# One order of steps for a whole two-layer backbone: single PSUM banks in the first stage, and both plain output projections written as steps

## The chip, the cores and the metric

The kernel runs on one core of a Trainium2 chip. The core has a matrix engine (TensorE, "PE" in the profile, with "PEld" for its weight loads), VectorE ("DVE"), ScalarE ("ACT"), GpSimd ("POOL"), and queues that start transfers; most of them are issued by the core's sync engine ("SP"). The on-chip memory SBUF holds tiles of 128 partitions; the matrix engine writes to PSUM, which has eight banks of 128 x 512 float32 numbers. The metric is the device time of one execution in microseconds, and fewer is better.

## The reference: what is computed

512 latent tokens and 256 context tokens, 1024 wide, pass through two layers. Layer 0 mixes tokens by windowed attention (16 query heads and 4 key/value heads of width 64, a sink logit per head, a band of 384 keys and the 256 context keys). Layer 1 mixes them by a gated MLP over chunks of 128 tokens. Behind each mixer stands a SwiGLU feed-forward net (FFN) of hidden width 2816. Both halves of a layer stand between RMS norms and are modulated by six rows (shift, scale and gate for mixer and FFN), which come from SiLU of a conditioning vector times a 1024 x 6144 matrix. Shortened:

```python
mod_l = silu_c @ ada_w[i] + ada_b[i]           # six rows of 1024
h_l = modulate(rmsnorm(x, norm_g[i, 0]), sh_ml, sc_ml)
y_l = mixer(h_l, h_c)                          # layer 0: attention @ a_w_o, layer 1: (u * mixed) @ b_w_o
x = x + g_ml * rmsnorm(y_l, norm_g[i, 1])
f_l = swiglu(modulate(rmsnorm(x, norm_g[i, 2]), sh_fl, sc_fl), ffn_w_in[i], ffn_w_out[i])
x = x + g_fl * rmsnorm(f_l, norm_g[i, 3])
```

The context tokens feed only the keys and values of layer 0, since layer 1 does not read them.

## The kernel before

**Arithmetic.** Nearly every product is taken from halves: an operand is cast to a reduced format on ScalarE (`high`, line 403: "hi"), the rest is formed by a subtraction on VectorE or GpSimd (`low`, line 410: "lo"), and three matmuls hi x hi, hi x lo, lo x hi are added in PSUM. Weights come in 88 units of 1 MB (`Stream`, `ws`): `ws.fetch` brings a unit into one of two raw buffers, `ws.high` and `ws.low` form its halves in four pairs of tiles `w_hi`, `w_lo`.

**Stages.** First stage: the six token tiles (tiles 0 to 3 latent, 4 and 5 context) are loaded, normed and transposed (`turn_in`, line 683), shift and scale of the mixer are worked out per block of 128 channels (`ada0_rows`, `ada0_cols`), and keys and values are summed over eight such blocks (`kv`, line 763). Tables for the rotary embedding are loaded (`rope_in`) and transposed (`rope_turn`, line 904). Then the keys are copied out, rotated, transposed and split into halves (`k_copy`, `k_rope`, `k_add`, `k_turn`, `k_split`, lines 977 to 1018), the values are copied out (`v_copy`), and two of the eight query projections are made (`q_first`). Attention runs in 16 blocks of 128 queries and one key/value head; the other query projections, and the first half (four blocks of channels) of the output projection for token tiles 2 and 3 (`wo_high`, `wo_low`, `wo_part`), stand among them.

Then the output projection (`down`, line 1363): weight units 6 to 9, four token tiles, each with a chain behind it (`Chain`: square, rstd, gain, add to x, norm, shift, transpose) that leads to the hidden state H of the FFN. The FFN (`FFN`) makes its first two units plainly (`head`) and the other 20 as seven products of quarters in place of eight (`product`, line 1609; sums and differences of quarters by `diff` and `sum_a`). Its output matrix is done likewise (`seven`, line 1836: `product7`, `add7`, and `plain7` for what is left over). Layer 1 follows with the gated MLP (`v_part`, `u_part`, `mixed`), a second call of `down`, and the second FFN, whose end stores the result. Beside all this the modulation rows are summed on VectorE from chunks of the 1024 x 6144 matrices (`Ada`; in the names of the steps `m` and the row's number, 0 to 5, with `#2` where a name comes a second time, for layer 1).

**What sets the order of work.** Every engine takes its instructions in the order in which the program issues them. Most of the program is given as named steps, `at(time, step, ...)` (line 780); `run_plan` (line 790) sorts the steps planned so far and issues them. A step whose name stands in the long list `ORDER` is issued at its place there; any other falls behind, by its time. Inside `tc.manual_schedule()` that order is kept; outside of it the framework's own planner sorts instructions by a simulated timeline. Before, two stretches lay outside: the loads of x for layer 0's residual, and in both calls of `down` the first two weight units (the halves of their weights, `staged` halves of their inputs, their matmuls and a generator `bg` that adds up one modulation row). A tile that is released and taken anew makes the new writer wait for the last reader.

**PSUM in the first stage.** Three slots of two banks (`slotA`) and two single banks (`bankA`) share the eight banks. A pair of token tiles has its keys and values in one slot, and the four heads' transposed keys of a pair take one slot.

## Time and profile before

| What | us |
|---|---|
| median of three runs | 1098.92 (1098.61 to 1098.96) |
| the profiled execution's own time | 1098.0 |
| its span | 1096.2 |
| TensorE busy | 1078.7 |
| VectorE busy | 943.3 |
| ScalarE busy | 607.7 |
| GpSimd busy | 260.6 |

The span runs from the first to the last instruction of the profiled execution; its own time lies 1.8 us above the span. Matmuls overlap, and the profile models their ends, so a gap between two of them shows only where it is longer than the overlap. In a row of a group stand the line, the engine, the operation, output <- inputs, shapes and count, then the busy time and the mean of one in ns, then the idle time before it and what ended it. In a row of a timeline stand the start, the time taken and the instruction, and in brackets the idle time before it.

### The profile page before, as it was taken

Reading aid. Unit: us, or ns where it says so; the run is one execution under the profiler, and the core shown is the slowest. Engines: PE = TensorE matmul, PEld = TensorE weight load, DVE = VectorE, ACT = ScalarE, POOL = GpSimd, SP = SyncE. Lnnn points to the kernel's source line nnn. Section 1 sums busy time; section 2 is a strip of 40 time slices with the busy share of each in tenths; the row PEclk is TensorE's granted clock in tenths of the full one; section 3 lists DMA queues with packets and bytes.
Section 4 is the critical chain, followed back from the end, with each engine's and each line's share of the span. In section 5 each row is a group of like instructions: output and inputs, shape, how many; then the busy total and the mean of one; then the engine's idle time right before and its main releaser. Section 6 shows DMA issues by size and latency. Waiting matters only on the chain.

```text
span 1096.2 us, 17751 instructions
## 1 busy us (share of the span) xinstructions
PE 1078.7 (98%) x6894; PEld 948.6 (87%) x6894; DVE 943.3 (86%) x1386; ACT 607.7 (55%) x1054; POOL 260.6 (24%) x268
## 2 busy tenths in 40 slices
PE   8999999999999999999999999999999999999997
PEld 5778777878899999998888888888999999998885
DVE  6798999859999999978988778878988888979975
ACT  6447778656645555555665434356555554555662
POOL 2417767525500000001322311007300000003400
PEclk9999999999999999999999999999999999999999
DMA  9746342433255655459953387651243344369811
GB/s 367 278 164 182 114 146 75 136 127 111 82 174 191 193 176 183 162 174 312 227 95 116 111 303 277 204 191 48 77 154 135 103 149 154 123 229 307 166 22 77
DMA packets 50393, 181.25 MB, mean 165 GB/s; under 512 B 5371, under 2 KB 9723, under 8 KB 39173
## 3 DMA queue, kind: packets, MB, share of 16 engines
q1 hardware_dynamic: 42756, 165.44, 43.5%
q0 software_dynamic: 7552, 14.68, 7.8%
q8 instruction: 54, 0.88, 0.3%
q14 instruction: 31, 0.25, 0.1%
HBM read 171.71 MB, written 2.10 MB: 159 GB/s over the span
## 4 chain that ended last, share of the span: by engine, by line
PE 86%; DVE 7%; DMA 2%; issue 2%; ACT 1%; POOL 1%; SPq 1%; DVEq 0%; POOLq 0%; ACTq 0%
PE f L1618 35%; PE y L1802 14%; PE y L1829 5%; PE y L467 4%; PE v L467 4%; PE s_ps L1095 3%; PE pT_ps L1128 3%; PE o_ps L1144 2%; PE q_ps L856 2%; PE u L2038 1%; PE u L2036 1%; PE u L2037 1%; PE kv L459 1%; PE q L856 1%; PE kv L461 1%
## 5 line engine op out<-in xcount | busy, mean ns | idle before, releaser
L1618 PE MATMUL f<-H,w_hi 128*128 128x256 f32 x960 | 178.4, 284 | 1.1 <-DVE fc L1629 0.5
L1618 PEld LDWEIGHTS f<-H,w_hi 128*128 128x128 f32 x960 | 149.8, 192 | 2.2 <-DVE fc L1629 1.4
L1618 PE MATMUL f<-H,w_lo 128*128 128x256 f32 x480 | 135.8, 283 | 0.0
L1802 PE MATMUL y<-w_hi,s 128*128 128x512 f32 x448 | 120.1, 389 | 0.0
L1618 PE MATMUL f<-S,w_hi 128*128 128x256 f32 x640 | 118.7, 283 | 0.0
L403 ACT CAST w_hi<-w_raw 128x1024 fp32r<-128x1024 f32 x90 | 94.5, 1052 | 33.6 <-PE y L1802 7.8
L403 ACT CAST w_hi<-T 128x1024 fp32r<-128x1024 f32 x80 | 83.7, 1047 | 50.8 <-PE f L1618 33.2
L410 DVE TENSOR_TENSOR w_lo<-w_raw,w_hi 128x1024 fp32r<-128x1024 f32 (+1 forms) x81 | 96.3, 1198 | 7.8 <-ACT w_hi L403 5.8
L1625 ACT COPY fc<-f 128x256 f32<-128x256 f32 x120 | 44.8, 373 | 103.7 <-PE f L1618 101.2
L1618 PEld LDWEIGHTS f<-S,w_hi 128*128 128x128 f32 x640 | 99.9, 192 | 0.0
L1802 PEld LDWEIGHTS y<-w_hi,s 128*128 128x128 f32 x448 | 84.1, 188 | 17.4
L410 DVE TENSOR_TENSOR w_lo<-T,w_hi 128x1024 fp32r<-128x1024 f32 x80 | 97.4, 1217 | 0.0
L1618 PEld LDWEIGHTS f<-H,w_lo 128*128 128x128 f32 x480 | 92.1, 192 | 0.0
L1618 PE MATMUL f<-S,w_lo 128*128 128x256 f32 x320 | 90.7, 283 | 0.0
L1790 POOL DMA_DIRECT2D t<-in_w x48 | 42.3, 939 | 182.9 <-DMA t<-in_w 116.7
L583 POOL DMA_DIRECT2D acc<-acc x8 | 6.9, 866 | 313.0 <-DVE acc L569 307.2
L569 DVE SCALAR_TENSOR_TENSOR acc<-ada_k,sc,acc 128x1024 f32<-128x1024 f32 x56 | 71.6, 1279 | 7.5 <-DMA ada_k<-in_ada 5.3
L1802 PE MATMUL y<-w_lo,s 128*128 128x512 f32 x224 | 69.0, 389 | 0.0
L1618 PE MATMUL f<-H,x 128*128 128x256 f32 x480 | 64.2, 283 | 0.0
L467 PE MATMUL y<-w_hi,st 128*128 128x512 f32 x224 | 62.4, 391 | 0.0
L1618 PEld LDWEIGHTS f<-S,w_lo 128*128 128x128 f32 x320 | 61.4, 192 | 0.3 <-DVE w_lo L410 0.3
L1618 PEld LDWEIGHTS f<-H,x 128*128 128x128 f32 x480 | 60.5, 192 | 0.1
(257 smaller groups left out, 2750.0 us busy)
## 6 DMA issues: line engine op xcount, KB each, us to landing
w_raw<-in_w SPq DMA_DIRECT2D x67, 1024.0 KB, 5.9
ada_k<-in_ada SPq DMA_DIRECT2D x56, 512.0 KB, 4.6
ada_raw<-in_ada SPq DMA_DIRECT2D x12, 1024.0 KB, 4.9
w<-in_w SPq DMA_DIRECT2D x12, 1024.0 KB, 9.3
t<-in_w POOLq DMA_DIRECT2D x48, 256.0 KB, 5.9
ada<-in_ada SPq DMA_DIRECT2D x8, 1024.0 KB, 8.4
t<-in_w SPq DMA_DIRECT2D x8, 1024.0 KB, 13.6
w_raw<-in_w SPq DMA_DIRECT2D x10, 512.0 KB, 4.1
```

The costliest lines, as they stand in the source:

```text
L403: nc.scalar.copy(out=hi, in_=src)
L410: (eng or nc.vector).tensor_tensor(out=v(lo), in0=v(src), in1=v(hi).bitcast(F32), op=ALU.subtract)
L467: nc.tensor.matmul(dst, l, w[:, n * 512:(n + 1) * 512], start=first and i == 0, stop=last and i == 2)
L569: nc.vector.scalar_tensor_tensor(out=self.acc, in0=self.raws.pop(k), scalar=sc[:, k:k + 1], in1=self.acc, op0=ALU.mult, op1=ALU.add)
L856: nc.tensor.matmul(q_ps[p], w, HA[:, x, :], start=k == 0 and i == 0, stop=k == KC - 1 and i == 2)
L1095: nc.tensor.matmul(dst, q, keys, start=i == 0, stop=i == 1)
L1128: nc.tensor.transpose(ps[:, j * P:(j + 1) * P], self.probs[j][:, i * P:(i + 1) * P], ident)
L1618: nc.tensor.matmul(dst, l[:, w], r[:, k, :], start=first and k == 0 and j == 0, stop=k == 3 and j == 2, skip_group_check=True)
L1625: nc.scalar.copy(out=self.c[n][:, i * 256:(i + 1) * 256], in_=self.ps[n, 1 if i == 1 else 0])
L1790: nc.gpsimd.dma_start(out=self.tt[:, p * D + 512 * i:p * D + 512 * (i + 1)], in_=a["w"][F2[self.layer] + 1 + 2 * p + i][:, c:c + 512], acc ...
L1802: nc.tensor.matmul(self.bank7(i, j), st[:, c:c + P], w[:, z * 512:(z + 1) * 512], start=i == 1 and p == 0 and l == 0 and z == 0, stop=p == ...
L1829: nc.tensor.matmul(self.y[t][n], st[:, x + t * P:x + (t + 1) * P], parts[h][w][:, n * 512:(n + 1) * 512], start=v == 0 and h == 0 and i == ...
```

## The change

**Single banks.** `slotA` goes; all first-stage PSUM tiles are single banks, eight of them. Keys and values of a token tile have a bank of their own, `k_copy` and `v_copy` work on one token tile, and `k_turn` and `k_split` on two heads.

**Both output projections as steps.** In `down` the weight halves, the halves of the inputs (`stage_hi`, `stage_lo`), the matmuls and the loans of buffers become steps with names; the generator `shift_sums` becomes steps too. One manual schedule now spans the whole program; `keep` and the inner ones go. The loads of x become steps.

**Kept halves.** For the first projection the four blocks whose halves `wo_high` and `wo_low` had written into `HA` are read from there by all token tiles (`ready`), and the weight halves of its first two units (`cut=2`) are those of the attention stage. `HA` moves from the attention pool into a pool of its own, `hh`, with one buffer, which the hidden states of the FFNs, the gated MLP and the tile `t7` use after it.

**A new order.** The list grows from 3219 to 3317 names; 3211 stand in both, and of these at most 1812 keep their order to one another. The second FFN's twenty units keep their order. In the new list the rope tables come at the very start, the first FFN's units interleave, and the last products and the last chains stand in another order.

The diff, cut to its core; of the list only the first rows, those of the keys' transposes, some from the end of the first FFN's units, and the end are shown:

```diff
 ORDER = """
-x_fetch_5 square_in_5 rstd_in_5 norm_in_5_1 warm_0 warm_1 norm_in_5_0 x_fetch_4 square_in_4 rstd_in_4 norm_in_4_1
-norm_in_4_0 warm_2 warm_3 warm_4 dma x_fetch_0 square_in_0 x_fetch_1 turn_in_4_1 rstd_in_0 norm_in_0_0 turn_in_4_0
+warm_0 rope_in x_fetch_5 square_in_5 rstd_in_5 norm_in_5_0 warm_1 norm_in_5_1 warm_2 warm_3 x_fetch_3 square_in_3
+rstd_in_3 norm_in_3_1 dma rope_turn_0 rope_turn_1 x_fetch_4 norm_in_3_0 square_in_4 rstd_in_4 norm_in_4_0 norm_in_4_1
...
+k_turn_4_1 k_turn_0_1 k_add_2 wlow_3_1_0_512 q_cos_0 k_turn_0_0 k_turn_2_1 q_rows_1 q_sin_0 q_add_0 k_split_0_1
+q_high_0_0 q_low_0_0 q_swap_1 v_copy_4 q_sin_1 k_split_0_0 k_turn_2_0 k_split_2_0 q_cos_1 k_split_4_1 k_turn_4_0
+k_split_2_1 q_add_1 v_copy_5 k_split_4_0 q_high_0_1 q_low_0_1 q_high_1_0 q_high_1_1 q_low_1_1 q_low_1_0 wfetch_4
...
+f0product_18_2 f0part_low_18_1 m1add_chunk_2 f0up1_16 m0stack f0silu_16_0 f0silu_17_1 f0silu_16_1 m0total_0_slot
+m0total_512_slot f0keep_18_0 f0diff_19_2 f0part_high_19_1 f0gates_16 f0part_high_19_2 f0diff_19_4 f0part_low_19_1
+f0product_18_5 f0keep_18_1 f0product_18_6 m1fetch_chunk_3_spare m1add_chunk_3 f0gate1_18 f0silu_18_0 wfetch_30
...
+f0product_21_1 f0part_high_21_2 f0product_21_5 f0part_low_21_2 f0fetch7_11_1_big f0up1_20 f0up2_20 f0product_20_4
+f0silu_18_1 f0gates_18 m1halve_512 f0gate1_20 m0done_512 m1halve_0 f0keep_21_0 m1total_512_slot m1total_0_slot m5done_0
+f0fetch7_12_0_big f0gates_19 f0fetch7_11_0_raw m0done_0 m1done_0 m1done_512 f0keep_21_1 f0silu_20_0 f0product_21_6
...
-f1a7_low_4_3 f1product7_4_0 f1w7_high_4_2 f1a7_low_4_2 f1add7_p7d_1 f1w7_high_4_3 f1w7_low_4_2 f1add7_c22_1
-f1product7_4_1 f1product7_4_2 whigh_86_1 f1w7_low_4_3 wlow_86_1 f1take7_18 wlow_86_0 f1product7_4_3 f1add7_c21_1
-f1take7_19 f1plain7_9_0 f1add7_c21_0 whigh_87_0 whigh_87_1 f1plain7_9_2 wlow_87_0 wlow_87_1 f1take7_20 f1take7_21
...
-c0rstd_y#4 c0add_x#4 c3square_y_0_512 c2add_x#4 f1plain7_9_1 f1plain7_10_1 c1square_y_0_512 c2store c3gain_y_0_512
-c0store c1gain_y_0_512 c1gain_y_512_1024 c1square_y_512_1024 f1plain7_9_3_(1,) c1rstd_y#4 c1add_x#4 c1store
...
+f1a7_low_4_1 f1w7_low_4_1 f1product7_4_0 f1product7_4_1 f1t7_add_2_21 f1a7_high_4_2 f1w7_high_4_2 f1add7_p7_0
+f1a7_low_6_3 f1a7_high_5_0 f1s7_S1_1 f1w7_low_6_3 f1w7_high_5_0 f1add7_p7_1 f1product7_6_2 f1t7_add_3_21 f1a7_low_5_0
+f1a7_low_4_2 f1set_split_9 f1a7_high_5_1 f1s7_S1_2 f1w7_low_5_0 f1w7_high_5_1 wfetch_86 f1product7_6_3 f1w7_low_4_2
+f1product7_4_2 f1a7_low_5_1 f1a7_high_5_2 f1s7_S1_3 f1w7_low_5_1 f1w7_high_5_2 f1save7_u3_0 f1save7_u3_1 whigh_86_0
+f1product7_5_0 f1a7_low_5_2 f1a7_high_5_3 f1w7_low_5_2 f1w7_high_5_3 wlow_86_0 whigh_86_1 f1product7_5_1 f1a7_low_5_3
+f1w7_low_5_3 f1take7_18 wlow_86_1 f1product7_5_2 f1product7_5_3 f1a7_high_4_3 f1a7_low_4_3 f1w7_high_4_3 f1w7_low_4_3
+f1add7_p7d_0 f1take7_19 f1product7_4_3 f1add7_c21_0 f1add7_c22_0 f1plain7_9_2 f1take7_21 wfetch_87 f1add7_c12_0
+f1plain7_9_0 f1add7_c21_1 f1plain7_9_3_(0,) whigh_87_0 wlow_87_0 f1take7_20 f1add7_p7d_1 whigh_87_1 wlow_87_1
+f1plain7_10_0 c0square_y_512_1024 c0square_y_0_512 f1plain7_10_2 c2square_y_0_512 f1plain7_10_3_(0,) c0gain_y_0_512
+c0rstd_y#4 c0gain_y_512_1024 c2square_y_512_1024 f1add7_c12_1 c2gain_y_0_512 c2rstd_y#4 c0add_x#4 f1add7_c22_1 c0store
+c2gain_y_512_1024 f1plain7_9_1 c3gain_y_0_512 c3square_y_0_512 c2add_x#4 f1plain7_10_1 c1square_y_0_512
+c1square_y_512_1024 c2store c1gain_y_0_512 c1rstd_y#4 c1gain_y_512_1024 c1add_x#4 c1store f1plain7_9_3_(1,)
 f1plain7_10_3_(1,) c3square_y_512_1024 c3rstd_y#4 c3gain_y_512_1024 c3add_x_0_512 c3store_0_512 c3add_x_512_1024
 c3store_512_1024
 """.split()
...
+    hh = ctx.enter_context(pool("hh"))
+
+    def new_h(name="H"):
+        return hh.tile([P, 2 * KC, SEQ], F32R, name=name, tag="H", bufs=1)
+
+    HA = new_h("HA")
...
-    def slotA(name):
-        return psA_p.tile([P, D], F32, name=name, tag="b2", bufs=3)
-
     def bankA(name):
-        return psA_p.tile([P, 512], F32, name=name, tag="b1", bufs=2)
+        return psA_p.tile([P, 512], F32, name=name, tag="b1", bufs=8)
...
-        mm3(dst, lh, ll, whi, wlo, k == 0, k == KC - 1)
+        mm3(kv_ps[t], lh, ll, whi, wlo, k == 0, k == KC - 1)
...
-    def k_copy(t):
-
+    def k_copy(t, i):
+
+        if i == 0:
+            k_raw[t] = vec("ksrc") if t < NT else None
+            k_rows[t] = vec("kr") if t < NT else base.tile([P, D], F32, name="kr", tag="stg", bufs=4)
         if t < NT:
...
+            nc.scalar.copy(out=k_raw[t][:, i * 256:(i + 1) * 256], in_=kv_part(t + i, 0))
...
-        nc.scalar.copy(out=vals[:, t:t + 2, :, :], in_=kv_part(t, 1).rearrange("p t (h d) -> p t h d", h=KVH))
+        nc.scalar.copy(out=vals[:, t, :, :], in_=kv_part(t, 1).rearrange("p (h d) -> p h d", h=KVH))
...
-        dma(x[:, t, :], a["x"][t])
+        at(-110, dma, x[:, t, :], a["x"][t])
...
+        def stage_hi(k):
+            st = stage("st")
+            sts[k] = st[:, 0:512], st[:, 512:1024]
+            high(sts[k][0], lhs(k))
+
+        def stage_lo(k):
+            low(sts[k][1], sts[k][0], lhs(k))
...
         if not seven:
-            ws.unit(u0)
-            ready(0)
-            for v in range(nu - 2):
-                for t in range(NT):
-                    work(v, t)
-                ws.unit(u0 + v + 1)
-                ws.fetch(u0 + v + 2)
-                ready(v + 1)
-                run(bg, -(-left // (nu - 2 - v)))
...
+            for v in range(nu):
+                b = B + 12 * v
+                if v:
+                    at(b - 12.1, ws.fetch, u0 + v)
+                for h in range(2):
+                    if v >= cut:
+                        at(b + .4 * h - .9, ws.high, u0 + v, h)
+                        at(b + .4 * h - .8, ws.low, u0 + v, h, nc.vector)
+                    k = 2 * v + h
+                    if k not in ready:
+                        at(b + .4 * h - 1, stage_hi, k)
+                        at(b + .4 * h - .9, stage_lo, k)
+                if v < nu - 2:
+                    for t in range(NT):
+                        if v > 1 or t not in part:
+                            at(b + 3 * t, work, v, t)
...
-    down(WO0, 4, lambda k: staged(oT[k // 4][:, (k % 4) * 512:(k % 4 + 1) * 512]), lambda: V[0, 2],
-         lambda: (V[0, 4], V[0, 3], H0), f0.head, lend=f0.lend, part=part, first=f0.prepare, also=shift_row0)
+    down(WO0, 4, lambda k: oT[k // 4][:, (k % 4) * 512:(k % 4 + 1) * 512], lambda: V[0, 2],
+         lambda: (V[0, 4], V[0, 3], H0), f0.head, lend=f0.lend, part=part, first=f0.prepare, also=shift_row0,
+         ready={k: (HA[:, k, :], HA[:, KC + k, :]) for k in range(4)}, cut=2)
...
-    with tc.manual_schedule():
-        run_plan()
```

781 lines of the change are left out of this document (379 added, 402 removed).

## The prediction

> **What bounds the kernel now.** I read the page's busy line and chain first, then the table of busy time by stage, then the list of TensorE's waits, and only then single places in the timeline.
>
> ```profile
> span 1096.2 us, 17751 instructions
> PE 1078.7 (98%) x6894; PEld 948.6 (87%) x6894; DVE 943.3 (86%) x1386; ACT 607.7 (55%) x1054; POOL 260.6 (24%) x268
> PE 86%; DVE 7%; DMA 2%; issue 2%; ACT 1%; POOL 1%; SPq 1%; DVEq 0%; POOLq 0%; ACTq 0%
> ```
>
> TensorE is busy for 98% of the span and carries 86% of the chain. Its work (matmuls, transposes) is left as it is by the change, so the only thing an order can win is TensorE's idle time, 1096.2 - 1078.7 = 17.5 us. The table by stage says where that lies; its columns are the stretch, the busy time of PE, PEld, DVE, ACT and POOL, the clock, the DMA share and GB/s.
>
> ```profile
> 0.00:20.50 20.50, 16.88 (x96) 9.48 (x96) 12.86 (x36) 13.64 (x23) 4.78 (x11) 1.00 0.90 348
> 20.50:46.00 25.50, 25.25 (x227) 17.59 (x223) 17.96 (x41) 13.70 (x23) 11.21 (x15) 1.00 0.86 343
> 46.00:80.00 34.00, 32.91 (x158) 27.26 (x158) 29.35 (x43) 15.39 (x26) 6.06 (x8) 1.00 0.50 163
> 80.00:231.40 151.40, 149.23 (x993) 117.59 (x991) 133.24 (x271) 108.21 (x244) 101.27 (x116) 1.00 0.44 139
> 231.40:292.00 60.60, 59.81 (x284) 49.51 (x283) 50.51 (x68) 35.62 (x59) 31.84 (x22) 1.00 0.30 96
> 292.00:490.00 198.00, 196.86 (x1627) 195.64 (x1627) 192.67 (x264) 105.51 (x181) 3.62 (x4) 1.00 0.51 169
> 490.00:700.00 210.00, 210.00 (x1002) 176.41 (x1002) 171.97 (x217) 108.61 (x159) 46.63 (x45) 1.00 0.69 208
> 700.00:780.00 80.00, 79.75 (x388) 66.30 (x386) 69.63 (x94) 42.94 (x73) 31.06 (x21) 1.00 0.37 125
> 780.00:1066.00 286.00, 286.00 (x2040) 270.94 (x2041) 248.43 (x335) 156.50 (x248) 21.91 (x25) 1.00 0.50 153
> 1066.00:1088.10 22.10, 22.02 (x98) 17.89 (x96) 13.07 (x19) 6.55 (x16) 1.11 (x2) 1.00 0.07 26
> 1088.10:1096.20 8.10, 0.00 (x0) 0.00 (x0) 3.63 (x6) 1.05 (x4) 1.10 (x2) 0.74 0.49 191
> ```
>
> Idle by stage: head 3.6 us, first stage 1.3, attention 2.2, first projection 0.8, first FFN's quarters 1.1, second projection 0.25, tail 8.1; nothing from 490 to 700 and from 780 to 1066. The clock is full, so nothing is to be had there. Beside TensorE stands VectorE: 192.67 of 198 us in the first FFN, 88% in attention. Within the attention and FFN stretches an order can as easily lose as win.
>
> [...]
>
> The longest waits of TensorE, before an instruction:
>
> ```profile
> PE q_ps L856 <- DVE klo L410: 1.1, 1, 1.1
> PE hT L1346 <- DVE tmp L1339: 1.0, 2, 0.8
> PE s_ps L1095 <- DVE q_X L410: 0.6, 1, 0.6
> PE pT_ps L1128 <- DVE row L607: 0.5, 1, 0.5
> ```
>
> **The change part by part.** The sum is made against the profiled execution: span 1096.2, its time 1098.0, which lies 0.92 below the median of 1098.92.
>
> *The rope tables move to the head.* In the old order the 48 small transposes of the rope rows stand in the middle of the first stage; in the new one the rope's transfer is the second step of all, and the transposes follow the fourth of the five filler matmuls ("warm").
>
> ```profile
> 42.58 2.11 PE L910 MATMUL rope<-ident,rope 128*64 128x128 f32 x48
> 44.93 1.07 PE L712 MATMUL rows<-ada,s 128*32 128x256 f32 x16 [0.25 <-ACT ropeT L914]
> ...
> 16.09 1.07 PE L712 MATMUL rows<-ada,s 128*32 128x256 f32 x16 [0.20 <-DMA ada<-in_ada]
> 19.51 1.07 PE L712 MATMUL rows<-ada,s 128*32 128x256 f32 x16
> 20.51 0.50 PE L459 MATMUL kv<-w_hi,hc 128*128 128x512 f32 x1
> ...
> L675 PE MATMUL warm<-idle 128*128 128x512 f32 x10 | 6.9, 860 | 1.8 <-DVE idle L672 1.8
> rope<-in_rope SPq DMA_DIRECT2D x1, 192.0 KB
> ```
>
> They cost 44.93 - 42.58 = 2.35 us where TensorE is full. In the head they cost nothing: of the 16.88 us that TensorE is busy up to 20.5, 6.9 are filler, and the first k/v matmul at 20.51 waits for the modulation rows, which wait for a transfer (16.09). Without that cover the 2.35 us would come back. What the move does cost is its transfer: SP's queue puts 192 KB ahead of all x tiles and so ahead of that transfer, 0.197 MB at 348 GB/s = 0.56 us. Term: -2.35 + 0.56 = -1.8 us. Bounds: -2.35 (the transfer is hidden) and +0.6 (the head is late and the gain is lost further on).
>
> *Single banks in the first stage.* Three two-bank slots and two single banks become eight single banks. The k/v copies out of PSUM can start on a token tile alone, and k's transposes come in six halves. ScalarE gets more, smaller copies: the k copies of two latent pairs go from one to two each, the three v copies from one to two each, five instructions more.
>
> ```profile
> L1625 ACT COPY fc<-f 128x256 f32<-128x256 f32 x120 | 44.8, 373 | 103.7 <-PE f L1618 101.2
> L1135 ACT COPY pt<-pT_ps 128x512 f32<-128x512 f32 x40 | 23.1, 586 | 11.3 <-PE pT_ps L1128 10.8 <-PE o_ps L1144 0.3
> L410 DVE TENSOR_TENSOR klo<-kT,khi x6: 678/692/692, 76.7 to 84.1; 128x512 fp32r<-128x512 f32 x6
> ```
>
> One pair costs 2 x 373 - 586 = 160 ns more, five of them 0.8 us, hidden in the 18.6 us that ScalarE idles from 46 to 80; uncovered they would cost 0.8. In exchange the query projection that now waits 1.1 us for a split of k, and the score that waits 0.6 for the query halves, may wait for less. But that projection's bank must come free first, and which transposed half of k lay in it isn't to be seen. The best is -1.7. The worst is that it waits for the last of the six splits, 6 x 0.69 = 4.1 us. The old wait was for the second split, and the new order puts three of the six after the second query's rotation as well; I take half of the gain, -0.8.
>
> *Attention in a new order.* Nothing is added. Some modulation adds of the shift row stand up to four blocks later, where VectorE has more idle time. Idle now 2.2 us, of which 0.6 is counted above. I take -0.5, bounds -1.6 and +3 (twice the idle, lost by the same means).
>
> *First projection.* Four ScalarE casts and four VectorE subtractions go, since the halves of the first four blocks, kept for the second half of the tokens, now serve the first half too; of the eight of each these rows show, half stay.
>
> ```profile
> L403 ACT CAST st<-oT x8: 612/618/639, 227.6 to 243.8; 128x512 fp32r<-128x512 f32 x8
> L410 DVE TENSOR_TENSOR st<-oT,st x8: 674/685/1218, 228.2 to 245.4; 128x512 fp32r<-128x512 f32 x8
> ```
>
> That is 4 x 0.62 = 2.5 us of ScalarE and 4 x 0.69 = 2.7 of VectorE, but TensorE doesn't wait for them: in 60.6 us it idles 0.8, all in the wait of the transposes hT for the shift, well behind them. So nothing from the removal. The kept tile now outlives attention and shares its one buffer with the next hidden state; that one's first write comes after the first head chain, long after the last matmul that reads the kept halves. The new order puts the first FFN's opening products between the last head steps, which may fill the hT wait: -0.5, bounds -0.8 and +1.5. The x tiles, four transfers of 512 KB, are now steps too, two of them late; SP runs ahead of the steps, so I cost them at nothing, with the 1.5 above as the price if the weight transfers ahead of them block.
>
> *First FFN, nearly every step moved.* The old order is a strict pattern with 1.1 us of idle; the new one interleaves three units and leaves some sums of the modulation rows in their PSUM banks for up to nine units before they are read.
>
> ```profile
> L410 DVE TENSOR_TENSOR w_lo<-T,w_hi 128x1024 fp32r<-128x1024 f32 x80 | 97.4, 1217 | 0.0
> ```
>
> VectorE is 97% full (192.67 of 198) and gets no less work, so the best is -1.1. A product that finds no free bank waits for the reader of the oldest one, and ahead of that in VectorE's queue stands up to one subtraction of 1.217 us. After the two sums of the second row are made the new order opens eight more banks, with three held: 8 x 1.217 = 9.7 us at worst. The row nearest to it is the present idle of 1.1; I take +1.0, as much again.
>
> *Gating layer, second projection.* Idle 0.25 before; nothing added; 0, bounds -0.25 and +2. The second FFN keeps its order up to its last products: 0.
>
> *Tail.* The last matmul starts at 1087.63; the end is 8.1 us of ScalarE, VectorE and one store after it. Rows of ScalarE, VectorE and PE, from there on:
>
> ```profile
> 1085.17 0.60 ACT L430 ACTIVATE junk<-y 128x512 bf16<-128x512 f32 x1 [1.97 <-PE y L1829]
> 1087.77 0.60 ACT L430 ACTIVATE junk<-y 128x512 bf16<-128x512 f32 x1 [1.91 <-DVE tmp L1319]
> 1088.49 0.60 ACT L430 ACTIVATE junk<-y 128x512 bf16<-128x512 f32 x1
> 1085.80 1.88 DVE L1319 TENSOR_TENSOR tmp<-y,row 128x512 f32<-128x512 f32 x3
> 1088.49 0.21 DVE L439 TENSOR_SCALAR ry<-msy 128x1 f32<-128x1 f32 x1 [0.82 <-ACT junk L430]
> 1089.37 1.29 DVE L1323 SCALAR_TENSOR_TENSOR x<-tmp,ry,x 128x1024 f32<-128x1024 f32 x1 [0.66 <-POOL ry L440]
> 1090.57 0.21 DVE L439 TENSOR_SCALAR ry<-msy 128x1 f32<-128x1 f32 x1
> 1087.63 0.39 PE L1829 MATMUL y<-w_hi,st 128*128 128x512 f32 x1
> ```
>
> Token tile 1's second square waits 1.91 us at 1087.77 for the gain on the same half, which the old order puts ahead of it; so tile 1's rstd comes at 1088.49, its add ends at 1090.6, and the last tile's rstd, ready by 1089.2, starts at 1090.57. The new order has both squares of tile 1 in a row, then its gain and rstd. Worked forward: second square 1085.9, rstd 1086.6, add (0.88 behind the rstd, as above) 1087.5 to 1088.7, last square at 1088.1, done 0.7 later, last rstd 1088.85 in place of 1090.57: -1.7. From there to the end nothing changes. Bounds -1.9 and, with what follows, +1.4.
>
> ```profile
> L1819 DVE TENSOR_TENSOR y<-y,r 128x512 f32<-128x512 f32 x12 | 8.3, 694 | 1.1 <-PE y L1802 1.1
> ```
>
> Ahead of that the parts of product 4 now stand among those of 6 and 5, and tile 2's plain matmuls follow the last part at once; they wait for two adds into their banks, 2 x 0.69 = 1.4 us. The first bank is final half a part earlier, six matmuls at 210/1002 = 0.21 us, 1.3 us, so the adds are hidden but for 0.1; uncovered they cost 1.4.
>
> [...]
>
> Sum: -1.8 - 0.8 - 0.5 + 0 - 0.5 + 1.0 + 0 - 1.7 = -4.3 us; 1098.0 - 4.3 = 1093.7 for a profiled run, 1094.6 for the median.
>
> **The rivals.** *All listed idle goes:* every term at its lower bound, -2.35 - 1.7 - 1.6 - 0.8 - 1.1 - 0.25 - 1.9 = -9.7, 1089.2. For it: each of these stalls has a place of its own. Against: VectorE at 97% and 88%.
>
> *Only the tail is left:* the first stage reaches its end 2 us earlier and there waits for VectorE, which is busy 29.35 of 34 us from 46 to 80 with rotations, splits and weight halves; the later stages change nothing. -1.7, 1097.2. For it: the two longest waits in the list stand just there. Against: the modulation adds of that stretch wait for data, not for TensorE.
>
> *Slower, by held banks in the first FFN:* units 18 to 21, with the sums of three modulation rows parked, at 9.7 us in place of 1.0: -4.3 + 8.7 = +4.4, 1103.3. It decides from about 7.5 us on (5.3 gained elsewhere and 2.2 to be seen). For it: VectorE's 192.67 of 198. Against: ScalarE, which reads some of the banks, has half its time free there.
>
> *The order doesn't do what it says:* steps whose names the list doesn't hold fall behind it. The new names (halves of k, staging, the third row's adds) all stand in the list; 1 in 100, put with the slower case.
>
> **How the numbers follow.** About 0.2%, 2.2 us, is what a measurement of this kernel can tell from no change. The forecast has 0.52 (its own range 1091.5 to 1097; 0.05 of it lies within 2.2 us of before), all idle gone 0.14, only the tail 0.16, slower 0.18. Faster 0.47 + 0.14 = 0.61, same 0.16 + 0.05 = 0.21, slower 0.18. The range runs from a little below the best case, 1088.5, to the slower one, 1103.5; beyond it lie those parts of the first FFN and of k's bank that add up.
>
> **What would show it.** Rope: the 48 transposes start before 10 us, the first k/v matmul lies between 20 and 21.1, and the first stage ends 1.8 us earlier. Banks: the wait for klo at the first query projection of attention is gone or shorter. First FFN: PE idle there at most 2 us; waits of f for DVE that add up to 5 or more would make me wrong, and slower. Tail: 6.3 to 6.6 us between the last matmul and the end. The prediction falls if attention loses more than 2 us, or if the stall at the end of k's transposes grows past 2.

## The result and the profile after

The changed kernel takes 1107.04 us (median of four, 1106.19 to 1109.65) beside 1098.76 for the kernel before: ratio 1.008, 95% interval 1.0067 to 1.0093. Timed again later on, beside other kernels, the ratio is 1.0097 (1.0083 to 1.011). I had forecast 1094.6, in a range up to 1103.5: wrong in sign and outside the range. The profiled execution took 1109.65, the longest of the four, so the places below add up to 11.7 us where the medians differ by 8.3.

Span, busy line and shares of the chain of the kernel after:

```profile
span 1107.9 us, 17798 instructions
PE 1083.6 (98%) x6894; PEld 950.1 (86%) x6894; DVE 941.2 (85%) x1382; ACT 602.5 (54%) x1055; POOL 264.1 (24%) x268
PE 76%; DMA 10%; DVE 8%; issue 3%; ACT 2%; POOL 1%; SPq 1%; DVEq 0%; POOLq 0%; ACTq 0%
```

TensorE's idle time grew from 17.5 to 24.3 us, and its busy time by 4.9, although the same 6894 matmuls run: some of them ran slower (in the place at 667, below, a u matmul every 0.43 us in place of 0.23). In the chain, transfers went from 2% to 10%. So the first hint is not VectorE but DMA (the transfers). Where the time is lost shows when the starts of the same matmuls are set side by side (us, from the two traces; the last column is the difference of the stretches that end there):

| up to | before | after | this stretch |
|---|---|---|---|
| last k/v matmul | 69.25 | 69.44 | +0.2 |
| first score | 84.43 | 83.34 | -1.3 |
| first projection's first matmul | 231.48 | 231.49 | +1.1 |
| first FFN's output product, first matmul | 496.17 | 499.08 | +2.9 |
| second projection, first matmul | 705.23 | 714.74 | +6.6 |
| second projection, last | 750.47 | 762.39 | +2.4 |
| last FFN's output product, first | 977.35 | 989.94 | +0.7 |
| last matmul | 1087.63 | 1101.00 | +0.8 |
| end | 1096.23 | 1107.89 | -1.7 |

The table by stage of the kernel after, in the stretches that matter (PE, PEld, DVE, ACT, POOL busy, clock, DMA share, GB/s), and TensorE's longest waits:

```profile
292.00:499.00 207.00, 203.05 (x1670) 201.04 (x1669) 196.19 (x268) 107.89 (x187) 2.65 (x3) 1.00 0.54 181
499.00:660.00 161.00, 161.00 (x735) 133.70 (x734) 132.09 (x167) 86.27 (x128) 39.66 (x39) 1.00 0.66 185
660.00:677.00 17.00, 13.25 (x47) 10.43 (x46) 10.49 (x18) 7.45 (x11) 2.91 (x3) 0.80 0.72 233
677.00:714.70 37.70, 37.70 (x199) 32.35 (x198) 30.84 (x36) 11.71 (x19) 3.87 (x4) 1.00 0.53 171
714.70:762.40 47.70, 46.06 (x207) 37.33 (x206) 39.16 (x49) 24.07 (x41) 8.88 (x8) 1.00 0.54 185
```

```profile
PE ada_ps L608 <- DVE acc_st L419: 3.7, 1, 3.7
PE f L1635 <- DVE fc L1646: 2.1, 2, 1.4
...
PE f L1635 <- DVE x L419: 1.8, 2, 1.5
PE s_ps L1099 <- ACT p L1110: 1.6, 4, 0.7
PE y L479 <- DVE st L419: 1.2, 1, 1.2
PE fa L473 <- DVE H L419: 1.2, 1, 1.2
```

Three things are to be seen. In the 17 us from 660 the clock is 0.80 and only 47 matmuls start (76 in as long a stretch before). The largest wait is one that the list of before didn't have at all: a modulation row's sum (`ada_ps`) waits for its operand. And the waits of f are there, but VectorE, at 196.19 of 207 us in the first FFN, is now less full than before.

The place at 667, row by row (VectorE, SP, GpSimd, TensorE of the kernel after), and the clock around it; below that, from the kernel before, the same fold, mirror and low half:

```profile
654.11 1.28 DVE L581 SCALAR_TENSOR_TENSOR acc<-ada_k,sc,acc 128x1024 f32<-128x1024 f32 x1
655.42 0.33 SPq L409 DMA_DIRECT2D row<-in_norm_g  x1
655.75 0.88 POOL L595 DMA_DIRECT2D acc<-acc  x1 [15.58 <-DVE mu L2029]
655.84 0.38 SPq L409 DMA_DIRECT2D w_raw<-in_w  x1
666.06 0.47 SPq L409 DMA_DIRECT2D acc<-acc  x1
670.09 1.22 DVE L419 TENSOR_TENSOR acc_st<-acc,acc_st 64x1024 fp32r<-64x1024 f32 x1 [3.46 <-ACT acc_st L412]
667.24 0.39 PE L2054 MATMUL u<-H,w_lo 128*128 128x512 f32 x1
671.37 0.80 PE L608 MATMUL ada_ps<-acc_st,ones 128*128 128x512 f32 x1 [3.75 <-DVE acc_st L419]
671.96 0.63 PE L2052 MATMUL u<-H,w_u 128*128 128x512 f32 x1
...
667.00:671.30 4.30, 0.62 (x3) 0.19 (x1) 1.21 (x1) 2.11 (x4) 0.00 (x0) 0.86 0.98 282
671.30:674.00 2.70, 2.63 (x6) 2.15 (x7) 2.67 (x8) 1.33 (x3) 0.00 (x0) 0.50 0.88 346
674.00:676.60 2.60, 2.60 (x7) 1.98 (x7) 0.81 (x5) 2.57 (x4) 0.44 (x1) 0.50 0.76 274
```

```profile
652.44 0.87 POOL L583 DMA_DIRECT2D acc<-acc  x1 [1.27 <-DVE acc L569]
656.55 0.47 SPq L400 DMA_DIRECT2D acc<-acc  x1
660.57 1.22 DVE L410 TENSOR_TENSOR acc_st<-acc,acc_st 64x1024 fp32r<-64x1024 f32 x1 [1.60 <-ACT acc_st L403]
```

The row's last add ends at 655.4; then half of the sum is added onto the other by a transfer that GpSimd starts (the fold, 655.75) and copied back by SP (the mirror, 666.06), which waits until the fold has landed. A row of 512 KB and weights of 1 MB are issued within 0.4 us of the fold. The matmul on the sum starts 3.9 us later than TensorE's pace of 0.23 us a matmul would have it (3.75 behind the modelled end of the one ahead); and afterwards TensorE runs at half clock for 5.5 us, a u matmul every 0.43 us in place of 0.23, which costs another 2.7. It isn't asked for earlier than before: 12.1 us behind the end of the row's last add, where the kernel before has 12.4. What grew is the way to its operand, from 9.7 us (last add to low half) to 15.9, and nearly all of that is the fold, which takes 10.3 us to land in place of 4.0. Before, SP issues nothing from 648.7 until the fold has landed.

The tail of the kernel after (ScalarE and VectorE) is as worked out: tile 1's two squares are in a row, its add follows, and the last rstd starts at 1102.21, 1.2 us behind the last matmul (1101.00) in place of 2.9:

```profile
1098.54 0.60 ACT L439 ACTIVATE junk<-y 128x512 bf16<-128x512 f32 x1 [1.38 <-PE y L1846]
1099.26 0.60 ACT L439 ACTIVATE junk<-y 128x512 bf16<-128x512 f32 x1
1100.89 1.29 DVE L1323 SCALAR_TENSOR_TENSOR x<-tmp,ry,x 128x1024 f32<-128x1024 f32 x1
1102.21 0.21 DVE L448 TENSOR_SCALAR ry<-msy 128x1 f32<-128x1 f32 x1
```

### The profile page after: what moved, and what is told of

Same layout as the page of the kernel before. It is cut to its first block, busy times and chain, and to the rows that moved or that the text cites. A ratio compares the mean times of both kernels' runs of the same rounds, so it can differ in the third digit from the quotient of the medians.

```text
span 1107.9 us, 17798 instructions
## 1 busy us (share of the span) xinstructions
PE 1083.6 (98%) x6894; PEld 950.1 (86%) x6894; DVE 941.2 (85%) x1382; ACT 602.5 (54%) x1055; POOL 264.1 (24%) x268
## 4 chain that ended last, share of the span: by engine, by line
PE 76%; DMA 10%; DVE 8%; issue 3%; ACT 2%; POOL 1%; SPq 1%; DVEq 0%; POOLq 0%; ACTq 0%
PE f L1635 31%; PE y L1819 13%; PE y L479 6%; PE y L1846 6%; DMA w_raw<-in_w 3%; DMA ada_k<-in_ada 2%; PE s_ps L1099 2%; PE pT_ps L1132 2%; PE o_ps L1148 2%; DMA ada_raw<-in_ada 2%; PE q_ps L861 1%; PE v L479 1%; PE fa L473 1%; DVE acc L581 1%; PE fa L471 1%
## 5 line engine op out<-in xcount | busy, mean ns | idle before, releaser
L1819 PEld LDWEIGHTS y<-w_hi,s 128*128 128x128 f32 x448 | 84.1, 188 | 17.5
L1126 POOL TENSOR_SCALAR p<-p,st 128x512 f32<-128x512 f32 (+1 forms) x64 | 57.1, 907 | 31.2 <-DVE st L1122 21.8
L1110 ACT ACTIVATE p<-s_ps,st 128x512 f32<-128x512 f32 (+1 forms) x64 | 47.3, 740 | 26.4 <-DVE st L1105 24.6
## 6 DMA issues: line engine op xcount, KB each, us to landing
ada<-in_ada SPq DMA_DIRECT2D x8, 1024.0 KB, 10.9
```

Source lines behind the costliest of these rows:

```text
L1110: nc.scalar.activation(out=p[:, 0:self.n], in_=self.s[j], func=AF.Exp, scale=-1.0, bias=self.st[:, 4 + j:5 + j], accum_out=self.st[:, 8 + ...
L1126: nc.gpsimd.tensor_scalar(out=p, in0=p, scalar1=self.st[:, 12 + j:13 + j], scalar2=1.0, op0=ALU.mult, op1=ALU.mult)
L1819: nc.tensor.matmul(self.bank7(i, j), st[:, c:c + P], w[:, z * 512:(z + 1) * 512], start=i == 1 and p == 0 and l == 0 and z == 0, stop=p == ...
```

## The experiments

Ratios are against the kernel before, run on the same chip in the same session. Edits are of the order's list unless said.

### The sum moved; the weights moved (gating layer)

```diff
 u_part_1_0 m4fetch_chunk_4
-m2total_512_slot wlow_49_0 m2done_512#2
+wlow_49_0
 ... u_part_0_0
+m2total_512_slot m2done_512#2
```

> The changed kernel, but in the gating layer the first half of the gain row's sum (m2total_512) and its reader stand behind the next u product (u_part_0_0) instead of ahead of it. Theory, a matmul put ahead of its operand: in the changed kernel TensorE stands still for 3.9 us at 667.2 because the folded sum's low half is written only at 671.3, and then runs at half clock until 676.9 (another 2.7 us). The u product is 24 matmuls of 0.226 us, 5.4 us, so the sum would be asked for at 672.6, after its operand is there: both losses go, 1107.04 - 3.9 - 2.7 = 1100.4 where the clock had dropped, 1103.1 where it had not; the wait for acc_st is at most 0.5 us. Rival, the whole stretch is late: ScalarE and VectorE are behind with the weights of the next units, so the same idle time comes back at the next product as a wait for weight halves; time 1106 to 1107.5.

Ratio 1.0111 (1.0085 to 1.0137), no gain; the median, 1108.99, lies above even the rival's time. The wait for the sum is gone, but the next product waits 2.6 us for weight halves: the rival's mechanism, at two thirds of the old wait. Second edit, the other way round:

```diff
-wfetch_49
 m2add_chunk_7 ... m2fold#2 m2mirror#2
+wfetch_49
```

> The changed kernel, but the transfer of the third u unit's weights (1 MB) stands behind the mirror of the gain row's sum instead of ahead of its last add. Theory, the fold's transfer is slow because it shares the DMA engines: 256 KB took 10.3 us beside this 1 MB and a 512 KB row in the changed kernel, 4.0 us in the kernel before. With the 1 MB behind it the fold takes 4 to 6 us, the folded sum's low half is ready by about 667, TensorE's wait is under 0.7 us and the clock stays full: 1100.4 to 1103.1, as in the run with the sum moved. Rival, the fold is slow by itself or by its place on GpSimd's queue: it still takes about 10 us and the time stays at 1106 to 1107.5. A third way: the weights come 4 us later than now and the u product of that unit waits for them, 1104 to 1108.

Ratio 1.0106 (1.0083 to 1.013), no gain; the median, 1109.26, is above all three forecasts. TensorE's wait in the first run, the fold's transfers in before, after and the second run (KB, us to landing), and TensorE's wait in the second run:

```profile
PE u L2062 <- DVE w_lo L427: 2.6, 1, 2.6
```

```profile
acc<-acc POOLq DMA_DIRECT2D x1, 256.0 KB, 4.0
```

```profile
acc<-acc POOLq DMA_DIRECT2D x1, 256.0 KB, 10.3
```

```profile
acc<-acc POOLq DMA_DIRECT2D x1, 256.0 KB, 7.4
...
PE ada_ps L615 <- DVE acc_st L426: 6.2, 1, 6.2
```

The fold does get faster with less beside it (10.3 to 7.4 us), in part as the theory has it, which expected 4 to 6; but now the weights share with the mirror, land at 672.8, and their cast stands in ScalarE's queue ahead of the sum's cast, so the sum is later than ever. One step moved by hand moved the stall to the next late thing. Over all profiles, the fold takes 7.4 to 10.9 us in the seven with the new order of this layer, and 3.5 to 5.3 in the ten with the old one, where its matmul never waits.

### The old order of the first FFN; transfers taken out of it

In the first run the units' steps, from the fourth unit's first product to the last row's sum, are sorted as in the old list; the second edits the code, so that of a row's eight chunks only the first is fetched and added eight times:

```diff
 def fetch_chunk(self, k, of=vec):
+    if (self.layer, self.s) in ((0, 5), (1, 0), (1, 1)) and hasattr(self, "one"):
+        self.raws[k] = self.one
+        return
-    self.raws[k] = of("ada_k")
+    self.raws[k] = self.one = of("ada_k")
```

> The changed kernel, but the units of the first FFN (from the fourth unit's first product to the last sum of the modulation rows) stand in the order of the kernel before. Theory: the new order of the units alone costs the 2.9 us by which the FFN's end is later; all four stalls of TensorE there (321, 340, 359, 455 us; 4.8 us together) go, VectorE's 6.0 us of waits for weight transfers go, and 1.8 us of stalls as in the kernel before come back: 1107.04 - 2.9 = 1104.1. Rival: what is gained here is waited for again later, in the gating layer, whose stall doesn't depend on TensorE: VectorE and the transfers set the time from there, 1106 to 1107.5.

> The changed kernel with the transfers of the three modulation rows in the first FFN cut down: of a row's eight chunks only the first is fetched, and all eight adds read that one (so the rows that come out are not the reference's). VectorE's and TensorE's work and every step's place stay; some 19 of 22 transfers of 512 KB, a third of the bytes that run there, go. Theory, sharing: the weights' transfers are late because they share the engines with the rows' (8 us from issue to landing at the three stalls, 5 elsewhere); with the rows gone they land in 4 us or less, VectorE's waits for them fall from 6 to 9 us to under 3, and TensorE loses under 2.5 us there: ratio 1.004 to 1.007. Rival, release: they are issued too late because the new order reads each raw tile's last half later (the queue waits 112 us in sum for w_lo there, 29 in before), whatever runs beside them: waits of 5 us and more stay, ratio 1.008 to 1.011.

The old order gives 1.0062 (1.005 to 1.0074), 2.0 us less than the changed kernel by its first ratio and 3.8 by its second; the theory's 2.9 lies between. The new order without the rows' transfers gives 1.0034 (1.0021 to 1.0046), 5.1 and 6.9 us less, just below the theory's range. VectorE's waits in the first FFN of the kernel after, and of the run without the rows' transfers; and, from the kernel after, one such stall (VectorE, then TensorE):

```profile
DVE T L1595 <- DMA w_raw<-in_w: 6.0, 4, 2.1
```

```profile
DVE T L1598 <- DMA w_raw<-in_w: 1.6, 1, 1.6
```

```profile
355.13 1.29 DVE L1595 TENSOR_TENSOR T<-w_raw 128x512 f32<-128x512 f32 x2 [1.62 <-DMA w_raw<-in_w]
358.10 1.28 DVE L581 SCALAR_TENSOR_TENSOR acc<-ada_k,sc,acc 128x1024 f32<-128x1024 f32 x1 [0.28 <-DMA ada_k<-in_ada]
360.63 0.68 DVE L419 TENSOR_TENSOR x<-w_raw,x 128x512 fp32r<-128x512 f32 x1
361.36 1.46 PE L1635 MATMUL f<-H,x 128*128 128x256 f32 x10 [1.55 <-DVE x L419]
```

An operand sum T of the next unit stands in VectorE's queue before its weights have landed; VectorE waits 1.62 us, is busy for 5.93 of the 6.3 us that follow (355.1 to 361.4), and 6 us later TensorE waits 1.55 for a low half behind it. The weights behind this stall were issued at 346.9 and took 8.1 us to land; without the rows' transfers they took 5.1. Kernels with the new order of this FFN and the rows' transfers show 5.5 to 9.4 us of such waits, those with the old order none, though single weight transfers take up to 7.3 us there too. From the first projection's first matmul to the FFN's output, the new order takes 267.0 to 272.5 us in six profiles, the old one 264.7 to 264.8 in ten others, and the new one without the rows' transfers 263.2. So the new order loses by the rows' transfers beside the weights'; without them it takes 1.5 us less than the old order does with them (the old order without them wasn't run). That the queue also issues later (the rival) was not excluded as a part, but with the rows' transfers gone nothing of it was left to see in the time.

### The second projection: two steps moved

```diff
+m4done_0#2
 m3add_chunk_1 m3add_chunk_2 work_0_0#2
-m4done_0#2
 stage_hi_2 wlow_52_1 m3fetch_chunk_7
-m3add_chunk_3 stage_lo_2
+stage_lo_2 m3add_chunk_3
```

> The changed kernel, but in the second plain projection the reader of the fifth row's sum (m4done_0) stands ahead of the third row's adds 1 and 2, and the low half of the second unit's first operand (stage_lo_2) ahead of add 3. Theory: TensorE's two stalls there (0.56 us at 723.0 for the reader that frees its bank, 1.41 at 727.1 for the low half) come from VectorE, which waits in these adds for transfers of 512 KB (0.5 and 1.9 us) with the two needed steps queued behind; both go, 1107.04 - 2.0 = 1105.1. Rival: the later adds delay the row itself, and its reader or the next low half makes TensorE wait as long: 1106.5 to 1107.5.

Ratio 1.0096 (1.0083 to 1.0109): nothing. Both stalls are gone where they were, and 1.4 us of others stand some 12 us later; the projection took 46.9 us (47.7 after, 45.2 before).

### Putting regions back

In six runs parts of the changed kernel's list went back to the old order: `gate_old` from the end of the first FFN's units to the second FFN's head, `restored` the first FFN's units too, `best1` also first stage and attention (with the rope in the head). The old list doesn't name the second projection's steps, so I had to order these by hand.

> The changed kernel, but everything from the end of the first FFN's units to the head of the second FFN (gating layer, second plain projection, second FFN's head) stands in the order of the kernel before; the third row's adds and the projection's staging, which the old list doesn't name, stand unit by unit as the old code issued them. Theory: the losses there are all the order's: 6.6 us at 667 to 677 (3.9 of standstill, 2.7 of half clock), 2.0 in the second projection, 1.2 at 782. Against the changed kernel that is 9.8 where the clock dropped and 7.1 where it didn't: 1097.3 to 1100 beside 1107.04, with TensorE's waits between 490 and 790 us under 1 us in sum. Rival: the weights and rows come late there because of what the first FFN leaves behind (its transfers end later), so waits of 2 us and more stay at acc_st or at weight halves: 1102 to 1106.

> The run before this one with the first FFN's units in the old order as well. What is left of the change: first stage, single banks, attention, first projection, first FFN's head, and the last products with the tail. Theory, by the sum of the places: 2.9 us less than with the gating part alone, and against the kernel before the tail's -1.7 with +0.5 for a wait in the last products: 1.2 us under before, ratio 0.9989 (0.998 to 1.0). Rival: losses don't add up, since VectorE carries a delay from one stage to the next: what is won in the FFN comes back later, ratio 1.002 or more.

> The run before this one with the first stage and attention in the old order too, but the rope's transfer at the head of the list and its 48 transposes ahead of the last filler matmul, as in the change; single banks and the new order of the transition to attention are kept. Theory: in the changed kernel the rope's 2.35 us are lost again by 69 us through two waits (0.6 for a weight half that GpSimd splits, 0.5 for a split of hc's counterpart HA) and a start that is 0.65 late, which are the new order's; the 1.1 won at the first query projection is lost inside attention through four waits of scores for ScalarE (1.6). With the old orders both stay: 1.8 + 1.1 less than the run before this one, ratio about 0.9965 of before. Rival: attention's pace is VectorE's (88% busy) and takes up any earlier start: the score matmuls start 1 to 3 us earlier and attention ends where it ended, ratio 0.998 to 1.0.

Ratios 1.0234 (1.0215 to 1.0253), 1.0166 (1.0152 to 1.018), 1.0175 (1.0159 to 1.019). All three missed, by my own list: I cast each unit's weights one unit too early, so ScalarE waited for transfers ahead of the operands (in `restored` it is busy for 1.68 of the 5.6 us from 740.6; TensorE's wait there):

```profile
PE y L486 <- ACT st L419: 10.3, 4, 4.9
```

The gating layer did come out as the theory said: in `gate_old`, where the new order of the first FFN still stands ahead of it, the way from the FFN's first output matmul to the last u matmul takes 207.8 us as before (214.1 after), with no wait of TensorE's from 495 to 700. So the layer's loss is its own order's and not what the FFN leaves behind. `restored2` and `best2` have the projection set right as I thought (`best2` also the old attention), `best4` nearer still to the old trace.

> The run called restored, with the second plain projection's steps set right: there I had asked for the weight halves of each unit one unit too early, so that ScalarE waited for transfers ahead of the operand's casts and TensorE lost 10.3 us. Now staging, adds and fetches stand where the trace of before has them. Theory: gating layer, first FFN and second projection cost what they cost before, the first stage and attention keep the 1.8 us that the profile of restored shows at 703 (703.38 beside 705.20), the tail keeps 1.7 and the last products lose 0.6: ratio 0.9973 (0.996 to 0.999). Rival: the new code's second projection, whose adds and staging are steps of the list, costs by itself 2 us and more: ratio 0.999 to 1.002.

> The run before this one with attention in the old order as well; first stage, single banks and the transition stay new. From the profiles so far: the new first stage and transition start the scores 2.0 us earlier than before (82.4 as the mean of seven profiles, 84.43 before), the old attention takes 145.4 from the first score to its last matmul and the new one 147.0 to 148.6: 1.6 or more less than the run before this one, ratio 0.9955 (0.994 to 0.998). Rival: attention ends by VectorE's work, whatever its order and start: no difference to the run before this one within 0.5 us.

> The run called best2 with two regions set nearer to the kernel before: in the second projection the fetches of the last two units' weights stand ahead of the third row's later fetches, the last mixing product's bias (whose reader frees the bank that TensorE waited 1.8 us for at 713) ahead of the row's adds, and the staging of the last operands ahead of the sums' halves; and the last products of the second FFN stand in the old order, with only the last chains new. Theory, by the sum of places in best2's profile: the second projection takes 49.4 us there and 45.2 in before, of which 3.5 come back; the last products' wait of 0.6 goes: best2's ratio 1.0019 less 4 us, 0.998 (0.997 to 1.0), under the kernel before. Rival: these stalls are VectorE's lateness, and a wait moved out of one place comes back at the next: ratio 1.0005 to 1.002.

Ratios 1.0027 (1.0017 to 1.0038), 1.0019 (1.0008 to 1.003), 1.0008 (0.9999 to 1.0017), none as the theories had it. Each still pays 4.2 to 4.4 us more than before in that projection alone (49.4 to 49.6 us beside 45.2), at places that move with each try; its longest wait in `best4`:

```profile
PE y L486 <- DVE m L2078: 2.2, 2, 1.7
```

Up to there `best4` was 4.2 us ahead of before (700.98 beside 705.23). The rival, that a wait moved comes back at the next place, held for my lists. That the old order can't be had in the new code was not shown.

### The rope alone, the tail alone, and both ends together

On the kernel before: the rope's transfer first and its transposes behind the fillers; the list from the sixth product's second part on in the new order; and, in the third, the first stage with single banks and its new list up to attention's first steps, with the new order of the last chains behind the last product. Everything between is the kernel before.

> The kernel before with one edit: the rope's transfer first of all, its 48 transposes in the head right behind the five filler matmuls, each half copied out at once. Theory, as predicted: 2.35 us of full TensorE time go from the middle of the first stage, 0.56 is lost to the transfer ahead of the modulation's: first k/v matmul at 20.5 to 21.1, last kv matmul 1.8 us earlier, total ratio 0.9984 (-1.8 us). Rival, as the changed kernel's trace suggests: the earlier end of the stage is waited for again, by VectorE (85% busy from 46 to 80) before the first query projection or within attention: last kv earlier by up to 1.8, first score or attention's last matmul unchanged, ratio 0.9995 to 1.001.

> The kernel before with one edit: its list from the sixth product's second part of the last FFN to the end in the new order. Theory, as predicted: 1.7 us less from the last matmul to the end (6.4 to 6.6 in place of 8.1 to 8.6), and 0.5 to 0.7 lost to one wait of the last products for a weight half: ratio 0.999 (-1.1 us), interval about 0.998 to 1.0. Rival: the gain of the tail is the last matmul's own lateness, and the end stays: ratio 1.0.

> The kernel before with only two parts of the change: the first stage with single banks, the rope's transposes in the head and the new order up to the first steps of attention; and the new order of the last chains behind the last product. Attention, both plain projections, both FFNs and the gating layer are the code and the order of before. Theory, by the sum of places: the scores start 2 to 3 us earlier (81.4 to 82.4 in seven profiles with this first stage, 84.43 before), the old attention keeps that, the tail gives 1.7: 3.7 to 4.7 us, ratio 0.9957 to 0.9966 (0.995 to 0.998). Rival: the earlier start is taken up behind attention, where in the runs so far the second projection lost what the first stage had won: ratio 0.999 to 1.001.

Rope alone: 1.0021 (1.0012 to 1.003), slower; neither my theory nor the rival held. Its 48 transposes run at 9.1 to 11.2, the transposes of x start behind them at 11.14 in place of 8.95, and the first k/v matmul starts at 22.21 in place of 20.51; the last at 69.85 in place of 69.25. `best1`, with eight single banks but the old order up to the last k/v matmul, does no better: 21.69 and 69.87. Tail alone: 0.9994 (0.9986 to 1.0003): the end comes 6.9 us behind the last matmul in place of 8.6, the forecast's 1.7, of which the last products take back 0.7. Its interval holds both my theory and the rival.

Both ends: **0.9971 (0.996 to 0.9982), 1094.44 us**, beside 1097.72 for the kernel before in the same session: faster than both kernels by a small but clear difference, in the forecast's range though not in its closer one, and outside the rival's. Page of this run, and its longest waits beyond the fillers:

```profile
span 1092.2 us, 17764 instructions
PE 1078.1 (99%) x6894; PEld 948.7 (87%) x6894; DVE 943.4 (86%) x1386; ACT 607.5 (56%) x1059; POOL 263.3 (24%) x268
...
PE 87%; DVE 6%; DMA 2%; issue 2%; SPq 1%; ACT 1%; POOL 1%; DVEq 0%; POOLq 0%; ACTq 0%
```

```profile
PE hT L1345 <- DVE tmp L1338: 0.8, 1, 0.8
PE s_ps L1094 <- DVE klo L417: 0.6, 1, 0.6
```

The last k/v matmul starts at 67.41 (1.8 earlier than before), the first score at 81.31 (3.1), the first projection at 228.76 (2.7), and this lead stands through 745 us of old order (977.35 to 974.44: 2.9). The last products take 0.6 of it back, and the tail makes it 4.0.

### The changed kernel once more

> The changed kernel itself once more, beside the next three on one chip. Ratio to before 1.007 to 1.011. In its profile the theory of late transfers expects the same places as in the five profiles of kernels that share its first FFN (VectorE waits 5.5 to 9.4 us there for weight transfers, TensorE loses 2.4 to 7.8 us against the old order's pace; the wait for acc_st in the gating layer 2.6 to 6.2) with other sizes, since the transfers' times differ from one execution to the next; a theory of a fixed lag of VectorE expects the same sizes as in its first profile: 4.8 us in the first FFN and 3.9 at acc_st, within 0.3.

Ratio 1.0097. The same places. In the first FFN the sizes differ: 6.2 us with its head in place of 2.9, where 4.8 us of stalls became 6.3 and one of them, 2.2 us long, was followed by a clock of 0.83 from 457.2 to 459.2 and of 0.50 from there to 461. There a fixed lag is excluded. At the sum (3.6 in place of 3.9) and in the second projection (2.1 in place of 2.4) the difference is too small to tell the two theories apart.

## Why the prediction was wrong, point by point

- **Gating layer, forecast 0 (-0.25 to +2): +6.6.** This is the step that failed most. "Nothing added; 0" priced the moved steps by their own work alone and left out the transfers that move with them. A row and a weight unit now start beside the fold of a row's sum, which lands after 10.3 us in place of 4.0; its matmul, asked for at the same distance from the last add, waits, and the stall cost 1.7 times its own length through the clock (3.9 us of standstill, 2.7 more at half clock). That the old order of this layer takes the loss away is shown by `gate_old`; that one of these transfers alone makes it isn't, since without the weights beside it the fold still took 7.4 us and the stall moved on.
- **First FFN, forecast +1.0 (-1.1 to +9.7): +2.9, in other profiles up to +7.8.** The size lies in the bounds, the mechanism was wrong. I let a product wait for a held bank behind one subtraction of VectorE's, with VectorE full. It was VectorE that waited (6.0 us), for weights whose transfer the rows' fetches slowed (8.1 us at one stall, 5.1 without them); without these the same order, with the same rows parked in banks, wins 1.5 us. So the rival "held banks" (0.18) had the sign and not the cause. Of my signs, TensorE's idle time here passed the 2 us allowed (3.95), while the waits of f for DVE, 3.9, stayed under the 5 that were to tell.
- **Second projection, 0 (up to +2): +2.4.** VectorE's row adds wait for transfers (0.5 and 1.9 us at the two stalls) with a needed low half queued behind them, for which TensorE waits 1.2. The forecast left them out, since "nothing added"; but the third row's adds became named steps in VectorE's queue. Moving two of these steps (`go_fix`) took both stalls away and brought others, so the cause of the whole 2.4 stays open.
- **Second FFN, 0: +0.7 at its head and +0.8 in the last products,** where a product waits 0.4 for a weight half; the adds I had feared there are hidden. Its units 2 to 4 did change their order, against what the description of the change says; only those from 5 on keep it.
- **Attention, -0.5 (-1.6 to +3): +1.1,** in waits of scores for ScalarE (1.6 us in four, 0.2 in one before). Single profiles scatter by as much as this (new order 147.0 to 149.0 us from the first score to the last matmul, old order 145.4 to 148.2), so the size isn't settled.
- **First projection, -0.5: nothing.** The wait for the shift (0.8 us before) is gone as expected, and what it gave doesn't reach the FFN's output.
- **Rope -1.8 and single banks -0.8: right in sum only.** In thirteen profiles with the new first stage the first score starts 0.3 to 3.1 us earlier than before, 2.3 in the mean, against the forecast's 2.6; in the profile after it is 1.1. "In the head they cost nothing" was wrong: with the rope in the head the first k/v matmul starts 1.7 us later in `rope_alone` and 1.2 in `best1`, and the last one no earlier than before. Since `best1` has the eight single banks, free banks alone don't make the transposes cheap; it takes the new order of the first stage, and which of its moves does it wasn't shown. Of the banks' term, `best1` shows 1.2 us between the last k/v matmul and the first score.
- **Tail, -1.7: right, with its mechanism,** 8.60 to 6.89 us. (The sign, 6.3 to 6.6 us, counted from the modelled end of the last matmul; from its start it would have been 6.9.)
- **A misreading that changed no term:** the rival "only the tail" has the two longest waits of the list at the end of the first stage. The second of them, hT for tmp, stands in the first projection.

The terms for the two ends sum to -4.3 by the forecast, and a kernel with these alone is 4.0 shorter in its profile and 3.3 in the median. The 4.0 has some luck in it, since of the thirteen profiles this one has the earliest first score. The likeliest case was right in sum for the two ends and wrong in giving zero to 250 us of reordered steps.

## What to carry to other kernels

A reordered stretch that has no idle time has nothing to win and everything to lose (the gating layer, 0 idle from 490 to 700 before, lost 6.6 us): price it by the slack of each moved wait (its operand's chain, and what is fetched at the same time), never at zero because nothing is added. Look for transfers first: in the first FFN, where VectorE was idle for 2.7% of the time before (192.67 of 198 us busy), its wait of 1.62 us for a late weight in `after` became, 6 us later, a stall of 1.55 of TensorE. Take the parts of a change whose gain can be read from one place, time them together, and leave the rest of the order as it is.

## What was not expected of the hardware

A standstill of TensorE can cost more than itself: the 3.9 us at the sum in `after` cost 6.6. Waits in the first FFN of two runs (the sums moved, then the projection's steps moved), with the clock of the next 2 us behind the first and of the next 4 us behind the second; and, from `best1`, the clock behind a wait of 2.05 us ahead of the second projection:

```profile
PE f L1643 <- DVE fc L1654: 2.0, 1, 2.0
...
455.90:458.00 2.10, 2.08 (x17) 2.08 (x18) 2.10 (x3) 1.68 (x4) 0.00 (x0) 1.00 0.85 269
```

```profile
PE f L1642 <- DVE fc L1653: 2.2, 1, 2.2
...
454.20:456.20 2.00, 2.00 (x13) 2.00 (x14) 2.00 (x3) 1.32 (x3) 0.00 (x0) 0.74 0.93 283
456.20:458.20 2.00, 2.00 (x11) 2.00 (x11) 1.97 (x3) 0.38 (x1) 0.00 (x0) 0.50 0.52 217
```

```profile
705.74:709.15 3.41, 2.58 (x5) 1.63 (x6) 3.41 (x4) 0.43 (x1) 0.00 (x0) 0.50 0.40 115
```

Thirteen waits of 2.2 us or more, in eight profiles, were read with the clock around them, and at all of them it fell. The clock is the lowest mean in a stretch of about 2 to 5 us behind the wait; the time at half clock is my estimate from these windows, for a clock that is either full or half, where they reach far enough:

| run | wait, us | clock behind it | at half clock, us |
|---|---|---|---|
| `after` | 3.75 | 0.50 | 6.8 |
| `total_late` | 2.6 | 0.72 | 3.4 |
| `fold_alone` | 6.2 | 0.50 | 6.8 |
| `fold_alone` | 2.8 | 0.59 | |
| `fold_alone` | 2.2 | 0.50 | |
| `ffn0_old` | 2.6 | 0.55 | 3.4 |
| `go_fix` | 4.1 | 0.50 | 3.4 |
| `go_fix` | 2.2 | 0.50 | 3.4 |
| `after_again` | 3.4 | 0.67 | 3.4 |
| `after_again` | 2.2 | 0.50 | |
| `restored` | 4.9 | 0.50 | |
| `gate_old` | 5.1 | 0.50 | |
| `gate_old` | 2.2 | 0.50 | 3.4 |

In five of them (`after`; 6.2 and 2.2 in `fold_alone`; `restored`; 5.1 in `gate_old`) the mean was 0.80 to 0.88 already over the stretch of the wait. Below 2.2 us the length doesn't decide: the clock stayed at 1.00 behind 2.0 us in `total_late` and 2.1 in `fold_alone`, and was 0.50 behind 2.05 in `best1`; in `gate_old`, with waits of 1.7 and 2.0 us between 711.7 and 717, it was 1.00 up to 714, 0.68 up to 717 and 0.50 up to 719. A transfer's time depends on its company just as much: the same 256 KB fold took 4.0 us in the kernel before, where SP issues nothing from 648.7 until it has landed, 7.4 beside a 512 KB row in `fold_alone`, and 10.3 beside such a row and 1 MB of weights in `after`.
